# Pool sums over 8 and 16 tokens by one running-sum scan in place of three or four doubling additions

## The chip, the cores and the metric

The kernel runs on one core of one Trainium2 chip. The metric is device time in microseconds (us), the median over runs of one launch. In what follows PE is the matrix engine, DVE the vector engine, ACT the scalar engine, POOL the GpSimd engine, and SP the engine whose queue issues most of the DMA transfers. L12 means line 12 of the kernel before; lines of the changed kernel behind the edit are nine higher.

## What is computed

One layer of a hybrid decoder step. 2048 prompt tokens and 8 sequences of 8 sampled tokens (2112 tokens, 1024 features) are normalised and multiplied by `w_in` into four groups of 1024 columns: pool input `v`, pool gate, LRU input and LRU gate. The LRU group runs a convolution of width 4 and a gated recurrence; the pool group, which the change concerns, subtracts each token from a causal mean over its window and applies a 256x256 matrix per channel group:

```python
POOL_WINDOWS = (2, 4, 8, 16)      # one window per group of 256 channels
...
ext = jnp.concatenate([buf, v], axis=1)              # 15 rows of state, then the tokens
cs0 = concat([zeros, jnp.cumsum(ext, axis=1)], axis=1)
hi = cs0[:, POOL_BUF + 1:POOL_BUF + 1 + T, c0:c1]
lo = cs0[:, POOL_BUF + 1 - w:POOL_BUF + 1 - w + T, c0:c1]
cnt = jnp.minimum(pos + 1, w)
outs.append((hi - lo) / cnt - xcur[:, :, c0:c1])
...
y = jnp.einsum('btgc,gcd->btgd', d, pool_w) * pool_scale
```

Both groups are multiplied by SiLU of their gates, go through `w_out`, are normalised again and are added to the input.

## The kernel before, in words

Channels lie on the 128 partitions and tokens along the free dimension. Every fp32 operand of a matmul is split into a high and a low part (`hi` by a copy on ACT, `lo` by a subtraction on DVE), and each product takes three matmuls. The tokens are cut into three macro chunks m = 0, 1, 2 of 704 tokens; m = 2 also holds the 64 sampled tokens, which with their state rows make its pool rows 839 long instead of 719. In each macro chunk the work goes by quads: (m, p, kind), p = 0 to 3, kind V (pool input), G (pool gate), U (LRU input), L (LRU gate). A quad is a 256-column piece of the input projection for both halves of the chunk.

For m = 0 a quad is computed plainly, in eight steps. For m = 1 and 2 it is computed by seven products of 12 matmuls (a fast form of 2x2 block multiplication), numbered pid 1 to 7. Each needs one operand made of weight blocks (`w1V_4` is the one for m = 1, kind V, pid 4) and one made of the chunk's inputs. The seven input operands X11, T1, T2, X22, X21, T3, T4 lie in the big tile `XN`; pid 1, 5, 6, 3, 2, 7, 4 read them in this order. T1 to T4 are sums and differences ("raw" parts, written by DVE into `XA` or into two tiles `t_0`, `t_1`), and each of the seven then needs its `hi` (ACT, L334 or L336) and its `lo` (DVE, L321) before PE can use it. All seven are made anew at the two passages from one macro chunk to the next (`transition`, L1338). The pids 1, 6, 7 and 4 of a quad accumulate into one PSUM bank called `a`, and DVE or ACT reads the bank out after each (evacuation, L1007 on DVE), so pid 4 cannot start before pid 7 has been read out.

The pool input of a quad V lands in two tiles `e` (one per 128 channels), with 15 older tokens in front. When a quad V is complete, `pool_chain` (L1075) forms the window sums on DVE: for a window w it adds the tile to itself shifted by 1, 2, 4, ... (`tadd`, L324), each addition into a tile `s` of its own; that is one, two, three and four additions per tile for w = 2, 4, 8, 16. Then L1107 makes the mean minus the token, ACT and DVE split it into `dh` and `dl`, and PE applies the group's matrix (`y`), whose result DVE multiplies with the gate (L1153).

The order of the instructions on every engine is written by a small planner in the kernel itself, at build time: a generator such as `pool_chain` yields the engine that its next piece needs and the piece's cost in us, and the planner places the pieces against its own clock between the steps of the projection (`one_slot`, `run_jobs`). A piece whose result is needed at once is placed by `force`, just ahead of the product that needs it (`need_x`, L1385, for the inputs; `need_w` for the weights). Each engine then executes its instructions strictly in that order. The costs that `pool_chain` yields therefore move other work as well, on all engines. The planner also counts the tiles `e`, of which there are six (`e_free`).

After the three chunks follows the output projection in a fixed order (from L1803), which the change leaves alone.

Of the kernel before, what the change touches and what calls it, by code (L numbers as in the profile page):

```python
# [14 lines left out]
ALU = mybir.AluOpType  # L15
# [14 lines left out]
PB = 15  # L30
# [43 lines left out]
def hymba_kernel(  # L74
# [27 lines left out]
    def t_free():  # L102
        return T_BUFS - t_live[0]
# [5 lines left out]
    e_live = [0]  # L109

    def e_free():
        return E_BUFS - e_live[0]

    def e_tile(name, dtype=F32):
        e_live[0] += 1
        return sb.tile([P, EW], dtype, tag="e", bufs=E_BUFS, name=name)
# [90 lines left out]
    V, G, AC = nc.vector, nc.gpsimd, nc.scalar  # L207
# [52 lines left out]
    def seq8(ap, base, stride, off, n):  # L260
        return ap[:, base:base + N_S * stride].rearrange("p (s t) -> p s t", t=stride)[:, :, off:off + n]

    def as8(ap):
        return ap.rearrange("p (s t) -> p s t", t=S_S)
# [55 lines left out]
    def tsub(out, a, b, eng=None):  # L320
        (eng or V).tensor_tensor(out=out, in0=a, in1=b, op=ALU.subtract)  # L321

    def tadd(out, a, b, eng=None):
        (eng or V).tensor_tensor(out=out, in0=a, in1=b, op=ALU.add)  # L324
# [21 lines left out]
    def blocks(kind, p):  # L346
        return [KINDS[kind] + 2 * p + j for j in range(2)]
# [583 lines left out]
    def load_small(m, kind, p):  # L931
        t = sb.tile([P, 2, 512], F32R, tag=kind, bufs=1, name=f"{kind}{m}_{p}")
        small[kind] = t
        flat = t.rearrange("p a b -> p (a b)").bitcast(F32)
        i = 0 if kind == "pw" else 1
        if m:
            nc.sync.dma_start(out=flat, in_=swd[:, i, p, :])
            return
        if (kind, p) not in small_raw:
            small_early(kind, p)  # L940
        r = small_raw.pop((kind, p))

        def work():
            yield "A", 0.62
            AC.copy(out=t[:, 0, :], in_=r)
            yield "V", 0.71
            tsub(t[:, 1, :], r, t[:, 0, :].bitcast(F32))
            t_done(1)
            yield "t", LAG
            yield "D", 0  # L950
            nc.sync.dma_start(out=swd[:, i, p, :], in_=flat)
        small[kind, "job"] = spawn(work(), rank=1)
# [99 lines left out]
    def quad_end(q):  # L1052
        at = clock["A"] + HOP
        if q[2] in "GL":
            spawn(silu_chain(q), at, rank=1)
        elif q[2] == "V":
            spawn(pool_chain(q), at, rank=1)
        else:
            for j in range(2):
                spawn(conv_chain(q, j), at, rank=2)  # L1060
# [14 lines left out]
    def pool_chain(q):  # L1075
        m, p, _ = q
        w = WINDOWS[p]
        L = PB + MW if m < LM else PB + PW + N_S * SP_ST
        c = L * 0.00122 + 0.05
        ds = []  # L1080
        for j, blk in enumerate(blocks("V", p)):
            E = Q[q]["dst"][j]
            yield "G", 0.3
            if m < LM:
                G.tensor_copy(out=hp[:, blk, :], in_=E[:, MW:MW + PB])
            else:
                op = sb.tile([P, N_S + 1, PB], F32, tag="op", bufs=1, name=f"op{blk}")
                G.tensor_copy(out=op[:, 0, :], in_=E[:, PW:PW + PB])
                G.tensor_copy(out=op[:, 1:, :], in_=seq8(E, PB + PW, SP_ST, S_S, PB))
                nc.sync.dma_start(out=o_pool[blk], in_=op)  # L1090
            S, sh = E, 1
            while sh < w:
                yield "?", lambda: e_free() >= 1
                yield "V", c
                dst = e_tile(f"s{blk}_{m}_{sh}")
                first = PB if 2 * sh == w else 2 * sh - 1
                tadd(dst[:, first:L], S[:, first:L], S[:, first - sh:L - sh])
                if sh > 1:
                    e_live[0] -= 1
                S, sh = dst, 2 * sh  # L1100
            yield "V", 0.92
            if m == 0:
                f = sb.tile([P, 16], F32, tag="df", bufs=1, name=f"df{blk}")
                V.tensor_tensor(out=f[:, :w - 1], in0=S[:, PB:PB + w - 1], in1=rcnt[:, :w - 1], op=ALU.mult)
            d, e = S[:, PB:PB + MW], E[:, PB:PB + MW]
            n = MW if m < LM else PW
            V.scalar_tensor_tensor(out=d[:, :n], in0=d[:, :n], scalar=1.0 / w, in1=e[:, :n],  # L1107
                                   op0=ALU.mult, op1=ALU.subtract)
            if m == LM:
                V.scalar_tensor_tensor(out=as8(d[:, PW:MW]), in0=seq8(S, PB + PW, SP_ST, PB, S_S), scalar=1.0 / w,  # L1110
                                       in1=seq8(E, PB + PW, SP_ST, PB, S_S), op0=ALU.mult, op1=ALU.subtract)
            if m == 0:
                tsub(d[:, :w - 1], f[:, :w - 1], e[:, :w - 1])
            ds.append(d)
            e_live[0] -= 1
        Q[q]["d"] = []
        prev = Q.get((m, p - 1, "V") if p else (m - 1, NG - 1, "V"))
        yield "?", lambda: not prev or prev.get("maps")
        if not m and not p:
            yield "?", lambda: t_free() >= 1  # L1120
        load_small(m, "pw", p)
        for j, d in enumerate(ds):
            yield "A", 0.78
            dh = e_tile(f"dh{m}_{p}{j}", F32R)[:, :MW]
            AC.copy(out=dh, in_=d)
            yield "?", lambda: e_free() >= 1
            yield "V", 0.9
            dl = e_tile(f"dl{m}_{p}{j}", F32R)[:, :MW]
            tsub(dl, d, dh.bitcast(F32))
            e_live[0] -= 1  # L1130
            Q[q]["d"].append((dh, dl))
        sums.add((m, p))
        yield "?", lambda: Q.get((m, p, "G"), {}).get("silu")
        yield "t", 1.5
        for c in range(2):
            for j in range(2):
                yield "P", lambda j=j, c=c: pool_map(q, j, c)

    def pool_map(q, j, c):
        m, p, _ = q  # L1140
        need_small("pw")
        pw = small["pw"]
        Y = z_psum(f"y{m}{p}{j}{c}")[:, :CW]
        cs = slice(c * CW, (c + 1) * CW)
        mm3(Y, [(pw[:, 0, 256 * k + P * j:256 * k + P * (j + 1)], pw[:, 1, 256 * k + P * j:256 * k + P * (j + 1)],
                 Q[q]["d"][k][0][:, cs], Q[q]["d"][k][1][:, cs]) for k in range(2)])
        blk = 2 * p + j
        g = Q[m, p, "G"]["dst"][j]
        if j and c:
            Q[q]["maps"] = True  # L1150

        def evac():
            V.scalar_tensor_tensor(out=g[:, cs], in0=Y, scalar=col(C_SCALE, blk), in1=g[:, cs],  # L1153
                                   op0=ALU.mult, op1=ALU.mult)
            if c == 1:
                if j == 1:
                    e_live[0] -= 4

                def store():
                    yield "t", MLAG  # L1160
                    yield "D", 0
                    nc.gpsimd.dma_start(out=mixed[:, blk, m * MW:(m + 1) * MW], in_=g[:, :MW])  # L1162
                    t_done(1)
                spawn(store(), clock["V"] + HOP)
        return [("V", 0.58, evac)]
# [359 lines left out]
    with tc.manual_schedule():  # L1525
# [132 lines left out]
        clock.update(V=2.0, A=2.0, G=1.0)  # L1658
        T[0] = 0.0
        spawn(pool_chain((0, 0, "V")), rank=1)  # L1660
        spawn(silu_chain((0, 0, "G")), rank=1)
        for j in range(2):
# [56 lines left out]
        for n, (qi, i, qp, pid) in enumerate(slots):  # L1719
            q = QUADS[qi]  # L1720
            m = q[0]
# [210 lines left out]
```

## Time and profile before

| what | value |
|---|---|
| three runs | 1164.01, 1159.36 and 1167.0 us, median 1164.01 us |
| the profiled execution: its own time | 1162.96 us |
| its span in the profile | 1161.3 us |
| granted PE clock, mean | 0.996 |
| PE busy | 1125.8 us (97%) |
| DVE busy | 839.6 us (72%) |
| ACT busy | 656.5 us (57%) |
| POOL busy | 156.2 us (13%) |

The profile is that of one execution; times inside it count from the start of its span. Busy time is the time in which an engine executed something. The waits of an engine name what ended each of its idle times. A matmul of 352 columns is listed with 0.32 us, but matmuls overlap: twelve of them, listed together with 2.12 us, start 1.95 us before the next twelve.

### The profile page before, as it was taken

The numbers are of one execution on the slowest core, as the hardware profiler recorded it, in microseconds if no ns is written. First come the engines' busy times: TensorE is split into PE (matmuls) and PEld (weight loads), VectorE is DVE, ScalarE is ACT, GpSimd is POOL, SyncE is SP. The second block draws the span as 40 slices with busy tenths as digits, with TensorE's granted clock in tenths as the row PEclk, the third lists the DMA queues.
The fourth block names the chain that finished last, engine by engine and source line by source line (L and its number), as shares of the span: only waits on it lengthen the run. The fifth ranks groups of instructions, "written<-read, shape, count | busy, mean of one in ns | idle before, by whom it ended". The sixth has DMA issues, their size and how long they took to land. (4 is left out here: it accounts for less than half of the span.)

```text
span 1161.3 us, 17773 instructions
## 1 busy us (share of the span) xinstructions
PE 1125.8 (97%) x6274; PEld 1053.5 (91%) x6274; DVE 839.6 (72%) x1341; ACT 656.5 (57%) x1113; POOL 156.2 (13%) x264
## 2 busy tenths in 40 slices
PE   7999999999999999989899999999999999999996
PEld 6999999999999999989899999899888888888875
DVE  6797694779957656579767676656576578778777
ACT  5378666687784737568464847374864242344232
POOL 4201101001101010101202010101000003211232
PEclk9999999999999999999999999999999999999998
DMA  9655976976977989997999999998789577776563
GB/s 328 232 210 212 348 263 257 359 283 210 361 279 270 334 301 335 373 367 268 346 308 398 363 362 368 347 339 276 223 227 266 160 209 214 205 230 195 163 182 126
DMA packets 177464, 322.10 MB, mean 277 GB/s; under 512 B 24736, under 2 KB 86432, under 8 KB 177376
## 3 DMA queue, kind: packets, MB, share of 16 engines
q1 hardware_dynamic: 173536, 303.67, 76.3%
q0 software_dynamic: 3840, 17.30, 3.8%
q8 instruction: 49, 0.80, 0.3%
q14 instruction: 39, 0.32, 0.1%
HBM read 218.51 MB, written 102.15 MB: 276 GB/s over the span
## 5 line engine op out<-in xcount | busy, mean ns | idle before, releaser
L149 ACT ACT_TABLE_LOAD x70 | 89.8, 1283 | 2.0 <-PEq L1911 0.8
L458 PE MATMUL p<-XN,s 128*128 128x512 f32 (+1 forms) x224 | 86.9, 388 | 0.4 <-DVE s L141 0.4
L457 PE MATMUL p<-XN,s 128*128 128x512 f32 (+1 forms) x224 | 86.8, 387 | 0.0
L456 PE MATMUL p<-XN,s 128*128 128x512 f32 (+1 forms) x224 | 86.8, 387 | 0.0
L1190 DVE SCALAR_TENSOR_TENSOR xs<-u,parT,xs 128x704 f32<-128x704 f32 (+1 forms) x72 | 67.8, 956 | 18.4 <-ACT xs L1179 18.2
L449 POOL TENSOR_TENSOR xr<-ac,xr 128x512 f32<-128x512 f32 x27 | 49.0, 1835 | 214.9 <-DVE ac L590 110.9
L1153 DVE SCALAR_TENSOR_TENSOR g<-y,parT,g 128x352 f32<-128x352 f32 x48 | 27.9, 581 | 52.8 <-PE y L251 52.6
L569 ACT ACTIVATE p<-ac 128x512 f32<-128x512 f32 (+1 forms) x32 | 18.8, 587 | 83.0 <-DVE ac L449 83.0
L251 PE MATMUL zL<-XN,wL 128*128 128x352 f32 x384 | 64.9, 325 | 0.6 <-DVE wL L321 0.6
L251 PEld LDWEIGHTS zL<-XN,wL 128*128 128x128 f32 x384 | 62.6, 188 | 1.1 <-DVE wL L321 1.1
L138 ACT CAST s<-a 128x512 fp32r<-128x512 f32 x48 | 28.6, 616 | 49.5 <-DVE a L449 37.1
L449 DVE TENSOR_TENSOR a<-a,a 128x512 f32<-128x512 f32 x48 | 33.0, 690 | 31.9 <-DMA a<-mixed 28.7
L1162 POOL DMA_DIRECT2D mixed<-g x24 | 13.1, 548 | 306.2 <-DVE g L1153 117.2
L457 PE MATMUL p<-XN,a 128*128 128x512 f32 x137 | 54.2, 396 | 0.0
L456 PE MATMUL p<-XN,a 128*128 128x512 f32 x137 | 54.2, 395 | 0.0
L458 PE MATMUL p<-XN,a 128*128 128x512 f32 x137 | 54.2, 395 | 0.0
L251 PE MATMUL y<-dh,pw 128*128 128x352 f32 x192 | 54.1, 323 | 0.0
L458 PEld LDWEIGHTS p<-XN,s 128*128 128x128 f32 x224 | 42.1, 188 | 10.3 <-DVE s L141 0.8
L457 PEld LDWEIGHTS p<-XN,s 128*128 128x128 f32 x224 | 42.1, 188 | 9.5
L456 PEld LDWEIGHTS p<-XN,s 128*128 128x128 f32 x224 | 42.1, 188 | 9.4
L251 PE MATMUL zV<-XN,wV 128*128 128x352 f32 x288 | 48.6, 324 | 0.0
L251 PE MATMUL zG<-XN,wG 128*128 128x352 f32 x288 | 48.2, 324 | 0.0
(341 smaller groups left out, 3134.2 us busy)
## 6 DMA issues: line engine op xcount, KB each, us to landing
a<-mixed SPq DMA_DIRECT2D x112, 256.0 KB, 3.9
mixed<-g POOLq DMA_DIRECT2D x48, 352.0 KB, 6.1
w2V<-wsd SPq DMA_DIRECT2D x28, 512.0 KB, 6.7
w2G<-wsd SPq DMA_DIRECT2D x28, 512.0 KB, 6.9
w2U<-wsd SPq DMA_DIRECT2D x28, 512.0 KB, 6.7
w2L<-wsd SPq DMA_DIRECT2D x28, 512.0 KB, 7.6
wsd<-XN SPq DMA_DIRECT2D x27, 512.0 KB, 5.0
w1V<-wsd SPq DMA_DIRECT2D x24, 512.0 KB, 6.8
```

The lines of the kernel that those rows point to most:

```text
L138: hi_eng.copy(out=hi, in_=src)
L149: nc.scalar.preload_act_table_set(name)
L251: nc.tensor.matmul(out, lhsT=lhsT, rhs=rhs, start=start, stop=stop)
L449: (eng or nc.vector).tensor_tensor(out=out, in0=a, in1=b, op=op)
L456: nc.tensor.matmul(out, lhsT=ah, rhs=wh, start=start and k == 0, stop=False)
L457: nc.tensor.matmul(out, lhsT=ah, rhs=wl, start=False, stop=False)
L458: nc.tensor.matmul(out, lhsT=al, rhs=wh, start=False, stop=stop and k == KT - 1)
L569: nc.scalar.activation(out=junk, in_=o, func=AF.Square, accum_out=st[:, g:g + 1])
L1153: V.scalar_tensor_tensor(out=g[:, cs], in0=Y, scalar=col(C_SCALE, blk), in1=g[:, cs], op0=ALU.mult, op1=ALU.mult)
L1162: nc.gpsimd.dma_start(out=mixed[:, blk, m * MW:(m + 1) * MW], in_=g[:, :MW])
L1190: V.scalar_tensor_tensor(out=xs, in0=E[:, k:k + n], scalar=col(C_CW + 8 * k, b), in1=xs, op0=ALU.mult, op1=ALU.add)
```

## The change

For the windows 8 and 16 the loop of additions is replaced by two instructions: a reduction adds the first window (the w tokens that end with the chunk's first), and a scan carries it on, adding at each token the one that enters the window and subtracting the one that leaves it. The pieces yield 2.0 us of DVE to the planner in place of three or four times about 0.93 us (1.07 us for m = 2). One tile `s` is taken in place of three or four. The windows 2 and 4 keep their additions.

```diff
-            S, sh = E, 1
-            while sh < w:
+            if w > 4:
                 yield "?", lambda: e_free() >= 1
-                yield "V", c
-                dst = e_tile(f"s{blk}_{m}_{sh}")
-                first = PB if 2 * sh == w else 2 * sh - 1
-                tadd(dst[:, first:L], S[:, first:L], S[:, first - sh:L - sh])
-                if sh > 1:
-                    e_live[0] -= 1
-                S, sh = dst, 2 * sh
+                yield "V", 2.0
+                S = e_tile(f"s{blk}_{m}")
+                V.tensor_reduce(out=S[:, PB:PB + 1], in_=E[:, PB + 1 - w:PB + 1], axis=mybir.AxisListType.X,
+                                op=ALU.add)
+                V.tensor_tensor_scan(out=S[:, PB + 1:L], data0=E[:, PB + 1:L], data1=E[:, PB + 1 - w:L - w],
+                                     initial=S[:, PB:PB + 1], op0=ALU.add, op1=ALU.subtract)
+            else:
+                S, sh = E, 1
+                while sh < w:
+                    yield "?", lambda: e_free() >= 1
+                    yield "V", c
+                    dst = e_tile(f"s{blk}_{m}_{sh}")
+                    first = PB if 2 * sh == w else 2 * sh - 1
+                    tadd(dst[:, first:L], S[:, first:L], S[:, first - sh:L - sh])
+                    if sh > 1:
+                        e_live[0] -= 1
+                    S, sh = dst, 2 * sh
```

With the other costs the planner places much of DVE's, ACT's and PE's work between about 200 us and 800 us in another order. On PE the products of the projection keep their order; the gate products (`r`, `i`) and the pool products (`y`) between them move by up to about a dozen products, and pid 4 of two V quads changes its place. In the middle chunk (m = 1, p = 1) pid 4 now follows directly on pid 7, where two products of the G quad stood between them; in the last chunk (m = 2, p = 1) it is the other way round. The places below matter most. All three are on DVE. The numbers behind the names count instances and differ between the two programs for the same thing; `wr1G` to `w1G` are steps that make weight operands.

The first is the passage from m = 0 to m = 1, around pid 3, 2 and 7 of the first V quad (the evacuations `e1V`, `d1V` and `a1V`). Before:

```order
L321 TENSOR_TENSOR XN<-XA,XN 128x1408
L321 TENSOR_TENSOR wr1G_21_2994<-wr1G_11_2990,wr1G_21_2994 128x512
L321 TENSOR_TENSOR w1G_5_3184<-wr1G_22_2996,w1G_5_3184 128x512
L321 TENSOR_TENSOR wr1G_11_2990<-wr1G_22_2996,wr1G_11_2990 128x512
L1007 TENSOR_TENSOR e_1_3145<-e1V_3170,e_1_3145 128x352
L321 TENSOR_TENSOR wr1G_12_2992<-wr1G_12_2992,wr1G_11_2990 128x512
L321 TENSOR_TENSOR w1G_6_3222<-wr1G_11_2990,w1G_6_3222 128x512
L1007 TENSOR_TENSOR e_1_3145<-d1V_3229,e_1_3145 128x352
L321 TENSOR_TENSOR w1G_3_3243<-wr1G_12_2992,w1G_3_3243 128x512
L321 TENSOR_TENSOR xl_0_3168<-xs_0_3015,xh_0_3167 128x704
L1007 TENSOR_TENSOR e_1_3147<-a1V_3149,e_1_3147 128x352
```

In the changed kernel, the same stretch:

```order
L321 TENSOR_TENSOR XA<-XA 128x2x352 x2
L1007 TENSOR_TENSOR e_1_3123<-e1V_3145,e_1_3123 128x352
L321 TENSOR_TENSOR XN<-XA,XN 128x1408
L1007 TENSOR_TENSOR e_1_3123<-d1V_3203,e_1_3123 128x352
L324 TENSOR_TENSOR wr1G_22_2970<-wr1G_21_2968,wr1G_22_2970 128x512
L321 TENSOR_TENSOR w1G_5_3159<-wr1G_22_2970,w1G_5_3159 128x512
L1007 TENSOR_TENSOR e_1_3125<-a1V_3127,e_1_3125 128x352
L321 TENSOR_TENSOR XN<-XA,XN 128x1408
```

The first row of the piece before is the last of the seven `lo` parts, T4's, which pid 4 reads; it stood ahead of all three evacuations. Now the sixth (T3's) stands behind that of `e1V` and the seventh (T4's) behind that of `a1V`.

The second place is the passage from m = 1 to m = 2, around the same evacuations of its first V quad. Before:

```order
L1190 SCALAR_TENSOR_TENSOR xs_1_5760<-u_1_5449,parT,xs_1_5760 128x704
L321 TENSOR_TENSOR XA<-XA 128x2x352 x2
L1007 TENSOR_TENSOR e_2_5780<-e2V_5808,e_2_5780 128x288
L1007 TENSOR_TENSOR e_2_5780<-e2V_5808,e_2_5780 128x8x8
L321 TENSOR_TENSOR t_0_5711<-XA,t_0_5711 128x704
L321 TENSOR_TENSOR t_1_5712<-XA,t_1_5712 128x704
L321 TENSOR_TENSOR XN<-XA,XN 128x1408
L1007 TENSOR_TENSOR e_2_5780<-d2V_5881,e_2_5780 128x352
L1007 TENSOR_TENSOR e_2_5783<-a2V_5786,e_2_5783 128x288
L1007 TENSOR_TENSOR e_2_5783<-a2V_5786,e_2_5783 128x8x8
L321 TENSOR_TENSOR XN<-t_0_5711,XN 128x704
L321 TENSOR_TENSOR XN<-t_1_5712,XN 128x704
```

In the changed kernel:

```order
L1199 SCALAR_TENSOR_TENSOR xs_1_5687<-u_1_5420,parT,xs_1_5687 128x704
L1007 TENSOR_TENSOR e_2_5746<-e2V_5773,e_2_5746 128x288
L1007 TENSOR_TENSOR e_2_5746<-e2V_5773,e_2_5746 128x8x8
L321 TENSOR_TENSOR XA<-XA 128x2x352 x2
L321 TENSOR_TENSOR XN<-XA,XN 128x1408
L1007 TENSOR_TENSOR e_2_5746<-d2V_5846,e_2_5746 128x352
L1007 TENSOR_TENSOR e_2_5749<-a2V_5752,e_2_5749 128x288
L1007 TENSOR_TENSOR e_2_5749<-a2V_5752,e_2_5749 128x8x8
L321 TENSOR_TENSOR t_0_5706<-XA,t_0_5706 128x704
L321 TENSOR_TENSOR t_1_5707<-XA,t_1_5707 128x704
L321 TENSOR_TENSOR XN<-t_0_5706,XN 128x704
L321 TENSOR_TENSOR XN<-t_1_5707,XN 128x704
```

The raw part of T3 (`XA<-XA`) moved from ahead of the evacuation of `e2V` to behind it, and the raw part of T4 (`t_0`, `t_1`) from ahead of the evacuation of `a2V` to behind it, so that all three steps of T4 follow that evacuation.

The third place is the last G quad of m = 1, where DVE evacuates `d1G` and `a1G` and also computes the norm of the next chunk's tokens (`tok`, L293 to L299; one of its steps waits for a root on ACT). Before:

```order
L324 TENSOR_TENSOR s_1_8_5250<-s_1_4_5246 128x704
L1007 TENSOR_TENSOR g_1_5076<-d1G_5218,g_1_5076 128x352
L1107 SCALAR_TENSOR_TENSOR s_1_8_5250<-s_1_8_5250,e_1_4919 128x704
L293 TENSOR_SCALAR tok<-tok 128x6
L296 RECIPROCAL tok<-tok 128x6
L297 TENSOR_TENSOR tok<-tok 128x6
L298 SCALAR_TENSOR_TENSOR tok<-tok 128x6
L299 SCALAR_TENSOR_TENSOR tok<-tok 128x6
L1007 TENSOR_TENSOR g_1_5077<-a1G_5078,g_1_5077 128x352
```

In the changed kernel:

```order
L1007 TENSOR_TENSOR g_1_5053<-d1G_5193,g_1_5053 128x352
L1095 TENSOR_REDUCE s_1_5244<-e_1_4923 128x1
L1097 SCALAR_TENSOR_TENSOR s_1_5244<-e_1_4923,s_1_5244 128x703
L1007 TENSOR_TENSOR g_1_5054<-a1G_5055,g_1_5054 128x352
L321 TENSOR_TENSOR w1L_7_5263<-wr1L_21_5080,w1L_7_5263 128x512
L293 TENSOR_SCALAR tok<-tok 128x6
```

The evacuation of `a1G` moved ahead of the norm's steps; between the two evacuations now stand the reduction and the scan (printed as SCALAR_TENSOR_TENSOR at L1097).

## The prediction

> **What bounds the kernel now.** First the busy line of PE, then the busy times by window.
>
> ```profile
> PE 1125.8 (97%) x6274; PEld 1053.5 (91%) x6274; DVE 839.6 (72%) x1341; ACT 656.5 (57%) x1113; POOL 156.2 (13%) x264
> ```
>
> ```profile
> 262.00:311.00 49.00, 48.28 (x296) 47.74 (x295) 46.55 (x60) 36.32 (x52) 5.87 (x9) 1.00 0.76 269
> ...
> 100.00:800.00 700.00, 685.60 (x4200) 680.55 (x4199) 502.46 (x732) 450.56 (x711) 74.15 (x180) 1.00 0.88 320
> ```
>
> The window rows give length, then busy time of PE, weight loads, DVE, ACT and POOL. PE bounds the kernel: of the 700 us in which all pool sums lie, it works 685.6 at the full granted clock (the 1.00 behind the engines). The change adds or removes no matmul, so it can move only the 14.4 us in which PE stands there, or add to them. DVE is busy for 502 of the 700 us, so most of its work is hidden; but at the first passage between macro chunks (262 to 311 us) it is busy for 46.55 of 49 us, and there its order counts. Next the waits of PE, with their totals, counts and longest.
>
> ```profile
> PE a1G L249 <- DVE g L1007: 2.2, 1, 2.2
> ...
> PE a2V L249 <- DVE XN L321: 2.2, 2, 1.9
> ...
> PE e2V L249 <- DVE XN L321: 1.0, 1, 1.0
> ...
> PE a1V L249 <- DVE e L1007: 0.7, 1, 0.7
> ```
>
> PE's waits for DVE in the stretch come to 2.2 + 2.2 + 1.0 + 0.7 = 6.1 us: one evacuation of the last G quad of m = 1, the inputs of the second passage, and one evacuation of the first. That is the most that a less loaded DVE can give back; the other 8 us end with DMA, ACT or at no releaser that is shown.
>
> **The change on DVE.** The groups of L324 are the additions; L1256 is the recurrence's scan over about the same length, once with its start value in SBUF; L581 and L579 are operations on one column. Each row ends in busy us and mean ns of one.
>
> ```profile
> L1256 DVE TENSOR_TENSOR_SCAN rg<-w,hh,ig 128x728 f32<-128x728 f32 x8 | 13.9, 1732 | 0.2
> L1256 DVE TENSOR_TENSOR_SCAN rg<-w,hh,ig 128x704 f32<-128x704 f32 x8 | 13.4, 1679 | 0.1
> ...
> L324 DVE TENSOR_TENSOR s<-e 128x718 f32<-128x718 f32 x12 | 10.8, 899 | 0.0
> ...
> L324 DVE TENSOR_TENSOR s<-s 128x704 f32<-128x704 f32 x12 | 10.6, 882 | 0.0
> ...
> L324 DVE TENSOR_TENSOR s<-s 128x716 f32<-128x716 f32 x8 | 7.2, 896 | 0.0
> ...
> L324 DVE TENSOR_TENSOR s<-e 128x838 f32<-128x838 f32 x6 | 6.2, 1035 | 0.0
> ...
> L581 DVE TENSOR_SCALAR st<-st 128x1 f32<-128x1 f32 x16 | 4.4, 273 | 0.5
> ...
> L579 DVE TENSOR_SCALAR st<-st 128x1 f32<-128x1 f32 x16 | 2.5, 154 | 0.5
> ```
>
> Removed are 8 x 3 additions or 4 each for m = 0 and 1 (two chunks, two tiles, windows 8 and 16): 4 x 3 + 4 x 4 = 28 at about 0.89 us, and for m = 2 2 x 3 + 2 x 4 = 14 at about 1.03 us: 24.9 + 14.4 = 39.3 us. Added are 12 reductions of at most 16 elements and 12 scans. No reduction of this kind stands in the trace; the one-column rows bound it at 0.15 and 0.27 us, and I take 0.2. The scan of 703 gets the row of 704 with a start value in SBUF, 1.68 us. From 704 to 728 it grows by 53 ns, 2.2 ns per element, so that of 823 takes 1.68 + 119 x 0.0022 = 1.94 us. No scan with an add and a subtract is in the trace: below, it might cost as much as an addition of that length (0.88 us), above, twice the scan of the rows (3.4 us); I take 1.68, the same operation with other arithmetic. Added: 12 x 0.2 + 8 x 1.68 + 4 x 1.94 = 23.6 us. DVE saves about 16 us, at the scan's bounds 26 or, when it doubles, minus 5. All of it lies beside PE's work, so it enters the sum only where PE waits for DVE. A scan is one piece of 1.7 us where evacuations could slip between additions of 0.9, so an evacuation that falls due behind it comes up to 0.8 us later; PE notices only where pid 4 follows directly on pid 7. The reduction reads the 15 older tokens that POOL wrote when the quad began, as the first addition did, so POOL's queue holds it no longer than before; SP issues the same loads, and fewer tiles `s` are in use.
>
> The scan's row is 1.90 times the addition's on the same 704 elements (1679 against 882 ns). [...]
>
> In the timeline an addition of 0.89 us lets its successor begin after 0.81:
>
> ```profile
> 502.87 0.89 DVE L324 TENSOR_TENSOR s<-s 128x712 f32<-128x712 f32 x1
> 503.68 0.69 DVE L321 TENSOR_TENSOR w1L<-wr1L,w1L 128x512 fp32r<-128x512 f32 x1
> ```
>
> So 18 instructions fewer save some 1.5 us less than their durations say, about 14 us. [...]
>
> **What moves, first passage.** PE's products and DVE's rows there:
>
> ```profile
> 305.39 2.11 PE L249 MATMUL a1V<-XN,w1V 128*128 128x352 f32 x12
> 308.22 2.21 PE L249 MATMUL a1V<-XN,w1V 128*128 128x352 f32 x12 [0.72 <-DVE e L1007]
> ```
>
> ```profile
> 299.50 1.62 DVE L321 TENSOR_TENSOR XN<-XA,XN 128x1408 fp32r<-128x1408 f32 x1
> ...
> 307.65 0.52 DVE L1007 TENSOR_TENSOR e<-a1V,e 128x352 f32<-128x352 f32 x1
> ```
>
> Pid 7 ends at 307.50, its evacuation at 308.17, and pid 4 begins at 308.22; T4's low part was ready at 301.12. In the changed order that part follows the evacuation. Of pid 4 only the first matmul (0.16 us) can run without it. So PE goes on 308.1 + 1.62 = 309.7 at the earliest: 2.2 us after pid 7, less 0.16, is 2.0 in place of 0.72. T3's low part, now behind the evacuation of pid 3, ends some 2.1 us after it, a product takes 1.95, which adds 0.2 to 0.4. Term: **+1.6 us**; below 0 if DVE's queue lets the part through early, above 2.7 if ACT's high part of T4 is late by another 1 us.
>
> **Second passage.**
>
> ```profile
> 554.92 2.05 PE L249 MATMUL e2V<-XN,w2V 128*128 128x352 f32 x11 [1.01 <-DVE XN L321]
> ...
> 562.64 2.11 PE L249 MATMUL d2V<-XN,w2V 128*128 128x352 f32 x12
> 564.59 0.33 PE L249 MATMUL a2V<-XN,w2V 128*128 128x352 f32 x1
> 566.78 2.05 PE L249 MATMUL a2V<-XN,w2V 128*128 128x352 f32 x11 [1.87 <-DVE XN L321]
> 569.56 0.40 PE L249 MATMUL a2V<-XN,w2V 128*128 128x352 f32 x1 [0.73 <-issue]
> 570.31 2.04 PE L249 MATMUL a2V<-XN,w2V 128*128 128x352 f32 x11 [0.35 <-DVE XN L321]
> ```
>
> ```profile
> 562.91 0.59 DVE L1007 TENSOR_TENSOR e<-e2V,e 128x288 f32<-128x288 f32 x2 [2.44 <-PE e2V L249]
> 563.42 1.68 DVE L321 TENSOR_TENSOR t<-XA,t 128x704 f32<-128x704 f32 x2
> 565.02 1.70 DVE L321 TENSOR_TENSOR XN<-XA,XN 128x1408 fp32r<-128x1408 f32 x1
> ...
> 569.37 1.69 DVE L321 TENSOR_TENSOR XN<-t,XN 128x704 fp32r<-128x704 f32 x2
> ```
>
> ```profile
> 562.49 1.37 ACT L336 CAST XN<-XA 128x1408 fp32r<-128x1408 f32 x1
> ```
>
> T3: now the evacuation of pid 3 (0.5), the raw part (1.7), ACT's high part (1.37) and the low part (1.65) follow one another, 5.2 us, while PE has a product of 1.95 and one matmul to do: a wait of 3.1 in place of 1.87, +1.2. T4: the evacuation of pid 7 (0.5), the raw part (1.6) and the first half of the low part (0.85, with 0.1 to hand over) make 3.05, less one matmul 2.9, in place of 0.73 + 0.35: +1.8. T1's low part (the 1.01) now stands a product earlier and costs nothing; T2's stands later, behind two other low parts, and comes about 0.2 late. Term: +1.2 + 1.8 - 1.0 + 0.2 = **+2.2 us**, between -1 (the parts run ahead after all) and +5 (ACT is late for T2 and T3 by 1.4 us each).
>
> **Evacuations and pid 4.**
>
> ```profile
> 508.10 2.21 PE L249 MATMUL a1G<-XN,w1G 128*128 128x352 f32 x12 [2.24 <-DVE g L1007]
> ```
>
> ```profile
> 505.51 0.89 DVE L1107 SCALAR_TENSOR_TENSOR s<-s,e 128x704 f32<-128x704 f32 x1
> ...
> 507.53 0.52 DVE L1007 TENSOR_TENSOR g<-a1G,g 128x352 f32<-128x352 f32 x1
> ```
>
> ```profile
> 620.78 2.17 PE L249 MATMUL a2V<-XN,w2V 128*128 128x352 f32 x12 [1.70 <-DMA w2V<-wsd]
> ```
>
> Between 505.51 and 507.53 DVE made a mean and the tokens' norm before it evacuated `a1G`; in the changed order a reduction and a scan (1.9 us) stand there, but three or four additions less stand ahead. The evacuation comes some 2 us earlier: **-2.0**, of 2.24 at most. The 1.70 us ended with the load of `w2V_4`, at a pid 4 directly behind pid 7; two products later, that load is no longer late: -1.7. The like pair now made in m = 1 costs at least the 0.7 of an evacuation and at most that 1.7; I take 1.2. Net **-0.5**.
>
> **Sum:** +1.6 + 2.2 - 2.0 - 0.5 = +1.3 us on a profiled execution of 1162.96 us (a span of 1161.3 and 1.7 around it), 1164.3 us. The median of the runs shown is 1.05 us above that execution; with the same sum it would become 1165.3. Between the two I predict **1165 us**: no change.
>
> **Rivals.** *The savings reach the end.* If DVE set the pace, its 14 us would come off: 1163 - 14 = 1149 us, faster by 1.2%. For it speaks the 95% at the first passage; against it that PE waits for DVE for 6.1 us in all. A milder form, in which all these waits go and the pair at 620.78 too, gives 1163 - 6.1 - 1.7 = 1155 us, still within 1%.
>
> *The passages are made on demand.* The mechanism of T3 and T4 takes hold of every combination: each then costs raw part, high part and low part, 1.7 + 1.37 + 1.65 = 4.7, less a product of 1.95, so 2.75 us, for four of them at two passages 22 us, less the 4 us of waits that stand there already: 1163 + 18 = 1181 us, slower by 1.6%. It decides from the point at which the low part of T1 or T2, too, stands behind the evacuation just before its use. The order shows this for T4 at both passages and for T3 at the second, not for T1 and T2; but DVE may arrive late at them.
>
> *The scan is no cheaper.* At 3.4 us a scan DVE would lose 5 us and stay at 73%; four evacuations wait up to 1.7 us longer behind a scan: 1163 + 1.3 + 4 x 1.0, about 1168 us, within 1%.
>
> **How the numbers follow.** About 1% (11.6 us) is what a measurement of this kernel can tell from no change; its three runs alone lie 7.6 us apart. Chances: the forecast 0.65; the mild relief 0.12; the scan no cheaper 0.08; the savings reach the end 0.06; passages on demand 0.09. Within 1%: 0.65 + 0.12 + 0.08 = 0.85; faster 0.06; slower 0.09. The terms' own bounds add up to -4 (0 - 1 - 2.2 - 1.0) and +9 (2.7 + 5 + 0 + 1.7), so 1159 to 1172 us; with 3 us more on either side for the place of a new median among runs 7.6 us apart, the range is 1156 to 1175 us. It leaves out the savings that reach the end, most of the passages on demand and the edge of the mild relief.
>
> **What would show it.** Right: 12 scans near 1.7 and 1.9 us; DVE busy about 825 us; PE busy within 1 us of 1125.8; the wait at `a1G` gone; waits of PE of 2 us for T4 at the first passage, and of about 3 us each for T3 and T4 at the second; no wait for `w2V_4` at 620. Wrong: a wait of PE over 3 us that is not at the passages; passages whose waits stay at 0.7 and 4; PE's idle time between 100 and 800 us below 8 or above 26 us.

## The result, and the profile after

The changed kernel takes 1168.54 us (median of 16 runs, 1164.68 to 1172.25) where before took 1163.1 us beside it (16 runs, 1157.85 to 1167.0): 1.0053 times as long, 95% interval 1.0037 to 1.0069. It is slower by half a per cent, some 6 us. The forecast was 1165 us and no change that can be told; the time lies inside the range, but the loss is four to five times the 1.3 us of the sum. The profiled execution of the changed kernel is the longest of its 16 (1172.25 us, span 1170.5 us), so what is read in it overstates the loss: 9.2 us of span against before's profile. Of all kernels below, two executions in a slower state (1226.6 us at price 2.5, 3453.5 us at price 0.8) are left out of medians and ratios.

The busy line of the page, after:

```profile
PE 1129.9 (97%) x6274; PEld 1056.9 (90%) x6274; DVE 823.9 (70%) x1323; ACT 651.1 (56%) x1108; POOL 165.9 (14%) x264
```

The new instructions by their lines (count, then shortest, median and longest duration in ns):

```profile
L1097 DVE TENSOR_TENSOR_SCAN s<-e,s x12: 1681/1682/1931, 154.4 to 770.9; 128x703 f32<-128x703 f32 x8, 128x823 f32<-128x823 f32 x4
L1095 DVE TENSOR_REDUCE s<-e x12: 150/154/167, 154.2 to 770.7; 128x1 f32<-128x8 f32 x6, 128x1 f32<-128x16 f32 x6
```

DVE does 15.7 us less (839.6 to 823.9), as the prices of the prediction said. In other pairs of profiles that differ by scan for additions alone it is 12.5 to 16.5 us, so the 16 us and the 14 us of the prediction can't be told apart. PE, which runs the same matmuls, is busy for 4.1 us more: some of its matmuls took longer. Where, the products of PE show. First passage, after (start, duration; in brackets the idle time ahead and what ended it):

```profile
298.89 0.32 PE L249 MATMUL a1V<-XN,w1V 128*128 128x352 f32 x1
300.41 2.05 PE L249 MATMUL a1V<-XN,w1V 128*128 128x352 f32 x11 [1.20 <-DVE XN L321]
...
309.52 0.40 PE L249 MATMUL a1V<-XN,w1V 128*128 128x352 f32 x1 [0.84 <-issue]
311.00 3.52 PE L249 MATMUL a1V<-XN,w1V 128*128 128x352 f32 x11 [1.09 <-DVE XN L321]
```

PE waits for T2's low part (1.20), then at pid 4 until pid 7 is read out (0.84; DVE ends that evacuation at 309.42), then for T4's low part (1.09); before there was one wait of 0.72. And the eleven matmuls at 311.00 took 3.52 us instead of 2.05. Second passage, after:

```profile
553.61 2.12 PE L249 MATMUL a2V<-XN,w2V 128*128 128x352 f32 x12
...
561.07 2.18 PE L249 MATMUL a2V<-XN,w2V 128*128 128x352 f32 x12 [1.43 <-DMA w2V<-wsd]
563.09 2.11 PE L249 MATMUL e2V<-XN,w2V 128*128 128x352 f32 x12
565.04 2.11 PE L249 MATMUL d2V<-XN,w2V 128*128 128x352 f32 x12
568.95 0.43 PE L249 MATMUL a2V<-XN,w2V 128*128 128x352 f32 x1 [1.80 <-ACT XN L336]
570.61 3.42 PE L249 MATMUL a2V<-XN,w2V 128*128 128x352 f32 x11 [1.23 <-DVE XN L321]
576.31 0.43 PE L249 MATMUL a2V<-XN,w2V 128*128 128x352 f32 x1 [2.29 <-ACT XN L334]
577.24 3.51 PE L249 MATMUL a2V<-XN,w2V 128*128 128x352 f32 x11 [0.50 <-DVE XN L321]
...
588.40 2.12 PE L249 MATMUL d2G<-XN,w2G 128*128 128x352 f32 x12
```

Here PE waits 1.80 + 1.23 = 3.03 us for T3 and 2.29 + 0.50 = 2.79 us for T4, and twice more eleven matmuls take 3.4 to 3.5 us. DVE at that place shows the new order: the raw part of T3 (565.81) stands behind the evacuation of `e2V`, and DVE was idle for 3.70 us before that evacuation.

```profile
565.31 0.59 DVE L1007 TENSOR_TENSOR e<-e2V,e 128x288 f32<-128x288 f32 x2 [3.70 <-PE e2V L249]
565.81 1.68 DVE L321 TENSOR_TENSOR XA<-XA 128x704 f32<-128x704 f32 x2
568.93 1.62 DVE L321 TENSOR_TENSOR XN<-XA,XN 128x1408 fp32r<-128x1408 f32 x1 [1.43 <-ACT XN L336]
```

The long matmuls stand where the granted clock is recorded at 0.50. Rows of 3.41 us, the length of each stretch at 0.50, after (length, busy time of PE, weight loads, DVE, ACT, POOL, then the clock):

```profile
307.47:310.88 3.41, 1.60 (x9) 1.10 (x7) 2.72 (x5) 0.62 (x1) 0.00 (x0) 1.00 0.34 126
310.88:314.30 3.42, 3.30 (x11) 3.30 (x12) 3.39 (x6) 0.00 (x0) 0.00 (x0) 0.50 0.95 266
314.30:317.71 3.41, 3.41 (x23) 3.41 (x22) 1.79 (x4) 2.46 (x5) 0.57 (x1) 1.00 0.84 238
...
566.88:570.30 3.42, 0.70 (x3) 0.19 (x1) 1.99 (x2) 1.36 (x1) 0.76 (x1) 1.00 1.03 414
570.30:573.71 3.41, 3.10 (x11) 3.11 (x11) 0.69 (x2) 0.00 (x0) 0.00 (x0) 0.50 1.01 404
573.71:577.12 3.41, 0.74 (x3) 0.22 (x2) 3.02 (x6) 1.56 (x2) 0.00 (x0) 1.00 0.65 184
577.12:580.54 3.42, 3.30 (x11) 3.30 (x12) 3.42 (x5) 0.00 (x0) 0.00 (x0) 0.50 0.18 71
```

Three times a row in which PE worked for 1.60, 0.70 or 0.74 us of 3.41 is followed by one at clock 0.50. Each costs 1.4 to 1.5 us (3.52, 3.42 and 3.51 in place of 2.05), 4.3 us together. In the profile of before the clock stays at 1.00 at both passages (250 to 320 and 540 to 600 us); around its longest wait there (1.87 us, for T3) PE worked for 1.94 us of a row:

```profile
565.31:568.72 3.41, 1.94 (x11) 1.75 (x11) 1.85 (x2) 0.60 (x1) 0.00 (x0) 1.00 1.02 418
```

How much a passage costs can be read in one number, since twelve products lie between the first product of the second passage and `d2G`: 588.40 - 553.61 = 34.79 us after, 580.03 - 551.62 = 28.41 us before, and 12 x 1.955 = 23.5 us if PE never waited (from 563.09 to 565.04, where it does not, the starts lie 1.95 us apart). Before:

```profile
551.62 2.12 PE L249 MATMUL a2V<-XN,w2V 128*128 128x352 f32 x12
...
580.03 2.12 PE L249 MATMUL d2G<-XN,w2G 128*128 128x352 f32 x12
```

Some of the other waits of PE, after, with total, count and longest:

```profile
PE a2L L249 <- DMA w2L<-wsd: 3.1, 2, 2.0
...
PE a2G L249 <- DMA w2G<-wsd: 1.7, 1, 1.7
PE p L458 <- DVE s L141: 1.4, 1, 1.4
PE a1G L249 <- DVE g L1007: 1.3, 1, 1.3
```

### The profile page after: what moved, and what is told of

The parts are those of the page before. It is cut to its first block, busy times and chain, and to the rows that moved or that the text cites. A ratio compares the mean times of both kernels' runs of the same rounds, so it can differ in the third digit from the quotient of the medians.

```text
span 1170.5 us, 17746 instructions
## 1 busy us (share of the span) xinstructions
PE 1129.9 (97%) x6274; PEld 1056.9 (90%) x6274; DVE 823.9 (70%) x1323; ACT 651.1 (56%) x1108; POOL 165.9 (14%) x264
## 5 line engine op out<-in xcount | busy, mean ns | idle before, releaser
L251 PE MATMUL zU<-XN,wU 128*128 128x352 f32 x288 | 48.4, 324 | 0.0
```

The source lines that it names most:

```text
L251: nc.tensor.matmul(out, lhsT=lhsT, rhs=rhs, start=start, stop=stop)
```

## The experiments

The theory to be tested: the scan costs nothing; the order that the planner makes of the new price costs, chiefly at the passages, and the waits there halve PE's clock. Rivals: the scan costs as one long piece on DVE; the clock falls whatever PE does; the order makes no difference. Ratios are to before, run beside each on the same chip. Beside the kernels of the experiments its median was 1160.4 to 1161.5 us, not 1163.1, so rows are to be compared by their ratios and not by their medians. "Clock" is the median over a kernel's runs of the mean granted clock (before: 0.995 over 86 runs; the change: 0.991 over 16). "Second passage" is the profile's time for the twelve products; with price 2.2 six short gate products lie among them, about 1 us, and in the filled kernels the matmuls that were added.

| kernel | median us | ratio, 95% interval | clock | second passage us |
|---|---|---|---|---|
| before | 1163.1 | 1 | 0.995 | 28.41 |
| the change | 1168.54 | 1.0053 [1.0037, 1.0069] | 0.991 | 34.79 |
| scan, order of before | 1164.46 | 1.0032 [1.0012, 1.0051] | 0.993 | 32.15 |
| additions, order of the change | 1174.46 | 1.0125 [1.0107, 1.0142] | 0.990 | 34.64 |
| the change, PE filled | 1165.85 | 1.0046 [1.0029, 1.0062] | 0.995 | 31.27 |
| sums left out, order of before | 1162.03 | 1.0014 [0.9996, 1.0032] | 0.994 | 28.39 |
| scan, price 1.8 | 1157.21 | 0.9970 [0.9950, 0.9990] | 0.996 | 33.76 |
| scan, price 2.2 | 1161.64 | 1.0002 [0.9987, 1.0017] | 0.993 | 34.42 |
| scan, price 2.5 | 1164.57 | 1.0020 [0.9999, 1.0040] | 0.994 | 33.68 |
| scan, three steps of 0.9 | 1150.67 | 0.9915 [0.9892, 0.9938] | 0.996 | 24.19 |
| additions, order of three steps | 1151.74 | 0.9921 [0.9899, 0.9942] | 0.996 | 24.15 |
| additions, price 0.8 | 1154.88 | 0.9941 [0.9920, 0.9963] | 0.995 | 25.92 |
| scan, order of before, PE filled | 1159.76 | 1.0003 [0.9983, 1.0022] | 0.995 | 28.41 |
| before, two instructions moved | 1159.93 | 0.9994 [0.9977, 1.0011] | 0.994 | 27.14 |

**The scan in the order of before.** The planner's steps stay; the pair (reduction and scan) is issued in the last one. In the traces every other instruction of PE, DVE, ACT and POOL stands in the same order as before.

```diff
             while sh < w:
                 yield "?", lambda: e_free() >= 1
                 yield "V", c
+                if w > 4:
+                    e_live[0] += 1
+                    if 2 * sh == w:
+                        e_live[0] -= 1
+                        S = e_tile(f"s{blk}_{m}")
+                        V.tensor_reduce(...)
+                        V.tensor_tensor_scan(...)
+                    if sh > 1:
+                        e_live[0] -= 1
+                    sh *= 2
+                    continue
```

> The scan in the order of before: the planner is asked for the three or four steps of before at their old price, and reduction and scan are issued in the last of them; all other instructions stand where they stood before, on every engine. Theory (the loss comes from the order that the single step of 2.0 gives): no slower than before, 1159 to 1163 us; DVE busy about 824 us; PE's waits 0.7 us at the first passage and about 4 us at the second, as before, and no window of half clock between 250 and 620 us. Rival (the scan itself costs, as one piece of 1.7 us that evacuations stand behind): 1166 to 1170 us, as the change.

Slower than before by 0.3%, 4 us against the before that ran beside it, and between the two expectations: DVE's relief brought nothing here, and neither answer is right as it stands. The profile shows where the relief went. DVE and PE of this kernel, ahead of the second passage:

```profile
511.49 0.69 DVE L324 TENSOR_TENSOR wr1U<-wr1U,wr1U 128x512 f32<-128x512 f32 x1 [5.25 <-DMA wr1U<-in_w_in]
```

```profile
504.10 2.22 PE L249 MATMUL a1G<-XN,w1G 128*128 128x352 f32 x12 [1.13 <-DVE g L1007]
...
515.56 2.84 PE L249 MATMUL a1L<-XN,w1L 128*128 128x352 f32 x12 [1.66 <-ACT g L1011]
518.19 3.06 PE L249 MATMUL a1U<-XN,w1U 128*128 128x352 f32 x12
```

and ACT:

```profile
512.26 0.62 ACT L845 CAST w1U<-wr1U 128x512 fp32r<-128x512 f32 x1 [5.46 <-DVE wr1U L324]
...
515.08 0.43 ACT L1011 COPY g<-a1L 128x352 f32<-128x352 f32 x1
```

`a1G` starts 4.0 us earlier than in before (504.10 against 508.10). But the raw weights `wr1U` do not come earlier by as much: DVE starts on them at 511.49, 2.8 us earlier than in before (514.32), and waits 5.25 us for them (1.63 in before), ACT behind it 5.46, the evacuation of `a1L` stands behind that on ACT, and PE waits for it 1.66 us (0.45 in before). At the second passage the lead is 1.3 us (`a2V` at 550.31 against 551.62). With the wait PE worked for 1.76 of the 3.42 us of a row, and in the next the clock was 0.53 in the mean. At the second passage a row with 1.79 us of work is followed by two at 0.50 and 0.53:

```profile
513.63:517.05 3.42, 1.76 (x11) 1.62 (x12) 3.38 (x6) 3.41 (x6) 0.00 (x0) 0.97 0.79 249
517.05:520.46 3.41, 3.41 (x14) 3.41 (x14) 2.92 (x5) 2.63 (x6) 0.00 (x0) 0.53 1.00 369
564.83:568.25 3.42, 1.79 (x10) 1.56 (x10) 2.43 (x3) 1.17 (x2) 0.51 (x1) 0.97 1.03 417
568.25:571.66 3.41, 2.56 (x8) 1.76 (x7) 2.10 (x4) 0.00 (x0) 0.00 (x0) 0.50 1.02 416
571.66:575.07 3.41, 3.41 (x14) 3.41 (x13) 3.41 (x5) 0.43 (x1) 0.89 (x1) 0.53 0.84 303
```

The second passage took 32.15 us in the same order in which before took 28.41. PE's waits there, 4.2 us, are hardly longer than before's 4.0; the row of before with 1.94 us of work was followed by clock 1.00. So of the 3.7 us at this passage some 3.5 are longer matmuls, and not longer waits.

**The sums left out.** As before, but the mean takes `E` in place of the sum and no addition or scan is made for windows 8 and 16.

> The order of before with no sums over 8 and 16 tokens at all: additions and scan are left out, and the mean is taken of the tokens themselves. DVE has 39 us less than before. Theory (DVE's work on the sums lies beside PE's): 1157 to 1163 us, at most the 6 us of PE's waits for DVE. Rival (DVE sets the pace where the sums stand): 1150 us or less.

DVE did 34 us less (805.2 us busy) and nothing came of it: 1.0014, with 1 in the interval. The rival that the savings reach the end is gone, for this order. The same loads hold it up again: DVE's idle time for `wr1U`, and PE's wait behind it, grew further:

```profile
512.41 0.69 DVE L324 TENSOR_TENSOR wr1U<-wr1U,wr1U 128x512 f32<-128x512 f32 x1 [6.92 <-DMA wr1U<-in_w_in]
```

```profile
516.48 3.89 PE L249 MATMUL a1L<-XN,w1L 128*128 128x352 f32 x12 [3.02 <-ACT g L1011]
```

**The additions in the order of the change.**

```diff
             if w > 4:
                 yield "?", lambda: e_free() >= 1
                 yield "V", 2.0
-                S = e_tile(f"s{blk}_{m}")
-                V.tensor_reduce(...)
-                V.tensor_tensor_scan(...)
+                S, sh = E, 1
+                while sh < w:
+                    ...
```

> The doubling additions in the order of the change: one step of 2.0 to the planner, and the three or four additions issued in it; all other instructions stand as in the change. Theory (the order costs): as slow as the change or slower, 1167 to 1175 us, since DVE is 16 us busier in the same order; the waits of PE at the second passage 7 us or more. Rival (the scan costs): 1163 us, as before.

1.25% slower than before: the order alone, with before's own additions, costs 14 us, and in it the scan ends 8 us earlier than the additions. So the scan does help where DVE is late; the largest single wait shows it (1.31 us in the change):

```profile
511.96 3.66 PE L249 MATMUL a1G<-XN,w1G 128*128 128x352 f32 x12 [4.59 <-DVE g L1007]
```

**PE filled.** Matmuls with a weight tile of zeros add nothing to the bank, but keep PE at work (18.70 of 20.00 us and 48.53 of 50.00 us in the two rows below).

```diff
+    FILL = {(1, 0, 'V', 6): (0, 6), (1, 0, 'V', 4): (0, 6), (2, 0, 'V', 6): (6, 0), (2, 0, 'V', 7): (9, 6), (2, 0, 'V', 4): (9, 2)}
+    ...
+    def fillers(out, n):
+        for _ in range(n):
+            mm(out, zero, xq("X11", 0, 0), False, False, True)
+
     def quad_product(...):
+        fillers(out, fill[0])
         for k in range(HK):
             mm(out, wh, xh, start and k == 0, False, chain)
+            if k == 0:
+                fillers(out, fill[1])
```

> The change, with 44 matmuls more on PE at the five places of the two passages where it waits: products with weights of zero, added to the bank that the next product uses (0.16 us each by the rows of 12 in 1.95 us, 7 us in all), so that PE works where it stood. Theory (the half clock of 3.4 us at the passages follows from PE standing about half of a window): the granted clock stays at 1.00 from 300 to 320 and from 550 to 600 us, the products there take 2.1 us again, and the end comes 2 to 4 us earlier than the change, 1164 to 1167 us. Rival (the clock falls whatever PE does): drops as in the change, and 1168 to 1172 us with what the added matmuls cost.

The clock does what the theory says at the passages, so the rival that it falls whatever PE does is gone. Stretches of this kernel:

```profile
300.00:320.00 20.00, 18.70 (x111) 17.56 (x110) 17.08 (x23) 8.04 (x14) 2.49 (x3) 1.00 0.76 267
550.00:600.00 50.00, 48.53 (x294) 47.18 (x293) 34.11 (x45) 20.87 (x39) 7.88 (x14) 1.00 0.92 324
```

Both passages run at 1.00, the second takes 3.5 us less than in the change, and the clock over its runs is back at before's 0.995 (in the profile a row at 0.50 stands behind them, 719.67 to 723.08 us, after one with 1.02 us of work in 3.41). In the total less is left: 1.0046 against 1.0053, intervals that overlap, so a gain in time is not shown. The 44 matmuls take PE about 7 us themselves (an estimate, 44 x 0.16, from twelve in 1.95 us), in place of waits and past them.

**The scan in the order of before, PE filled**, with ten such matmuls ahead of the wait at 515 us and eight inside T3's product.

```diff
+    FILL = {(1, 2, 'L', 2): (0, 0, 10), (2, 0, 'V', 7): (0, 8, 0)}
```

> The scan in the order of before, with 18 matmuls by weights of zero on PE: 10 behind the last product ahead of the wait at 515 us, 8 inside the product of T3 at the second passage. Theory (4 us were lost there, the larger half of it to two stretches of half clock): no stretch of half clock at 517 and 568 us, and 1161 to 1163 us, 2 us less than without them. Rival (the scan as a long piece on DVE costs it): 1164 to 1166 us.

Neither of the two stretches of half clock is left (the clock is 1.00 from 510 to 520 and from 560 to 576 us), and the ratio falls from 1.0032 to 1.0003. This kernel is as fast as before, with more on PE. That fits the reading that the clock took what the scan seemed to cost in that order, but does not prove it: the two intervals still overlap (1.0012 to 1.0051 and 0.9983 to 1.0022). The kernel's profiled run is one of its longest (1167.05 us), because of one load late by 4.69 us at 621 us.

**Other prices.** The one step's price is 2.0 in the change; here 1.8, 2.2 and 2.5, then three steps of 0.9 with the pair behind the third.

```diff
-                yield "V", 2.0
+                yield "V", 1.8
```

> The change with 1.8 in place of 2.0 as the one step's price to the planner, which gives another order; the same instructions in all. At the first passage the low parts of T3 and T4 stand ahead of the evacuations, as before; at the second they stand as in the change. Theory (the order costs, above all at the passages): between the two, 1162 to 1166 us, waits of the first passage 0.7 us again, those of the second 5 to 7. Rival (a price near the scan's true time is all that matters, or the one piece costs): as the change, within 2 us.

> The change with 2.2 as the step's price. At the first passage T4's low part stands behind the evacuations, as in the change; at the second the raw sums of T3 and T4 are made before the low parts of T1 and T2, ahead of where they stood in either kernel. Theory (the order costs): 1162 to 1167 us, waits of about 3 us at the first passage, under 5 at the second. Rival: as the change, within 2 us.

> The change with 2.5 as the step's price. Both passages stand as in the change, much else on PE stands otherwise. Theory (the passages carry the loss): as the change, 1166 to 1171 us, waits of 3 and 7 us, and stretches of half clock there. Rival (the loss is spread over the whole order, and passages are a part of it only): anywhere from 1158 to 1175 us.

> The change with three steps of 0.9 ahead of the reduction and the scan for either window. The first passage stands as before; at the second T4's raw sum is made ahead of T2's low part, earlier than in either kernel. Theory (the order costs, above all at the passages): 1159 to 1163 us, no more than before, waits of 0.7 us and of 4 us at most. Rival: as the change, 1166 to 1170 us.

In two of these expectations tiles are misnamed: at the second passage it is T3's raw part that stands ahead of T2's low part with three steps (T4's is next behind it), and with 2.2 the raw parts of T2 and T3 stand ahead of the low parts of T1 and T2.

The same instructions in five orders range from 0.9915 to 1.0053, with no trend by price. Price 1.8 came out below its range: its second passage is as bad as the change's (33.76 us), but at the first pid 4 stands behind two products of G and no wait is left: 21.56 us from the first `a1V` to `d1G`, 27.22 in the change. Price 2.5, with passages like the change's (27.27 us for 27.22 at the first, 33.68 for 34.79 at the second), missed its range by 1.4 us, so the rest of the order seems to have a part too. Price 2.2 had no wait at the first passage, pid 4 again standing behind two products of G, and lost 7.22 us in one wait for T1's low part at the second: both against its expectation, and the time within it. Three steps give the fastest kernel of all, 0.85% under before, and better than was expected. From 100 to 800 us PE stands 4.9 us in it, 14.4 in before and 18.3 in the change. Its second passage, PE and DVE:

```profile
558.91 2.11 PE L249 MATMUL d2V<-XN,w2V 128*128 128x352 f32 x12
560.86 0.33 PE L249 MATMUL a2V<-XN,w2V 128*128 128x352 f32 x1
561.36 2.05 PE L249 MATMUL a2V<-XN,w2V 128*128 128x352 f32 x11 [0.17 <-DVE XN L321]
563.24 2.10 PE L249 MATMUL a2G<-XN,w2G 128*128 128x352 f32 x12
565.18 2.12 PE L249 MATMUL e2G<-XN,w2G 128*128 128x352 f32 x12
567.14 2.12 PE L249 MATMUL a2V<-XN,w2V 128*128 128x352 f32 x12
```

```profile
552.53 1.69 DVE L321 TENSOR_TENSOR XA<-XA 128x704 f32<-128x704 f32 x2
554.14 1.69 DVE L321 TENSOR_TENSOR XN<-t,XN 128x704 fp32r<-128x704 f32 x2
555.74 1.69 DVE L321 TENSOR_TENSOR t<-XA,t 128x704 f32<-128x704 f32 x2
559.18 0.59 DVE L1007 TENSOR_TENSOR e<-e2V,e 128x288 f32<-128x288 f32 x2 [1.75 <-PE e2V L249]
559.68 1.62 DVE L321 TENSOR_TENSOR XN<-XA,XN 128x1408 fp32r<-128x1408 f32 x1
```

Both raw parts (552.53, 555.74) are made ahead of the evacuation of `e2V`, so that T3's low part follows that evacuation directly; and pid 4 comes two products of G after pid 7. One wait of 0.17 us is left, and the twelve products take 24.19 us.

**Whose gain is it?** The additions in that same order, and before with nothing but another price for its additions:

```diff
-                yield "V", c
+                yield "V", c if w <= 4 else 0.8
```

> The doubling additions in the order of the version with three steps of 0.9 (1150.7 us with the scan): all other instructions stand as there. It tells what the scan is worth in that order. If the order gives the gain: 1150 to 1155 us, faster than before all the same. If the scan gives it (16 us less on DVE): 1161 us or more. In the order of the change the same exchange was worth 8 us, in that of before nothing.

> Before, with nothing changed but the price of an addition for windows 8 and 16 told to the planner: 0.8 each in place of 0.93 (1.1 for m = 2). No scan. The first passage stands as before; at the second T4's raw sum stands ahead of T2's low part, as in the version with three steps. Theory (the second passage and the order at large carry the differences, scan or not): faster than before by 3 to 8 us, 1153 to 1158. Rival (the order is neutral and the scan gave the gain): 1161 us, as before.

The additions are as fast in that order as the scan (0.9921 and 0.9915, intervals that overlap almost wholly), with DVE 16 us busier. And a new price alone makes the kernel of before 0.6% faster, about 7 us: 2.5 of them at the second passage (25.92 for 28.41; T3's raw part is again the one that was meant), the rest elsewhere. The gain is the order's.

**Two instructions moved.** In before, the two instructions of T4's raw part are placed ahead of the evacuation of pid 3; all else stands.

```diff
         force(x_jobs[n])
+        if m == 2 and n == "X22":
+            while "T4" not in x_jobs:
+                run_jobs(T[0])
+                job = x_jobs["sums"]
+                if "T4" not in x_jobs and job["req"][0] == "V":
+                    grant(job, max(clock["V"], job["ready"], T[0]))
```

> Before, additions and all, with one thing changed: the two instructions of DVE that make T4's raw sum at the second passage stand ahead of the evacuation of pid 3 (where DVE stood idle for 2.44 us in before) and not behind it. Every other instruction stands as before on every engine. Theory (the place of the operands' instructions at the passages sets PE's wait there): T3's low part ends 1.6 us earlier, PE's wait for it falls from 1.87 to about 0.3 us, and the end comes 1.6 us earlier or more, 1157 to 1160 us where before has 1161. Rival (later gates take it back, as at 515 us): 1161 us.

```profile
562.73 0.33 PE L249 MATMUL a2V<-XN,w2V 128*128 128x352 f32 x1
563.71 2.04 PE L249 MATMUL a2V<-XN,w2V 128*128 128x352 f32 x11 [0.66 <-DVE XN L321]
...
617.79 3.51 PE L249 MATMUL a2V<-XN,w2V 128*128 128x352 f32 x12 [1.81 <-DMA w2V<-wsd]
```

The wait for T3 falls from 1.87 to 0.66 us and the passage from 28.41 to 27.14, so the place of these instructions does set that wait. The total, 0.9994, does not tell a gain of 1.3 us from none, and the expected 1.6 us are not shown in it. The load of `w2V` at the pid 4 of the next V quad ends a wait of 1.81 us, 1.70 in before, and here the twelve matmuls behind it took 3.51 us where they took 2.17 in before.

## Why the prediction was right, and where its sum was not

- **PE bounds, and DVE's saving lies beside it: right.** Taking the additions' price off DVE by the scan (12.5 us in that profile), or the sums altogether (34 us), in before's order moved the time by +0.3% and +0.1%; in the order of three steps the scan moved it by less than the interval. Only in the order of the change, where DVE is late, did it bring 8 us. The saving by itself therefore did not reach the end, and the kernel became slower by its order.
- **The prices: right.** Scans of 1.68 and 1.93 us (taken 1.68 and 1.94), reductions 0.15 (0.2), DVE at 823.9 us ("about 825").
- **First passage, +1.6 us: the step taken was right, the term too small.** The wait at pid 4 was foreseen at 2.0, the readout of pid 7 included, and is 0.84 + 1.09 = 1.93. That T2's low part would come late by 1.20 was not foreseen. Measured: 3.13 us of waits for 0.72, +2.4.
- **Second passage, +2.2 us: right for T3 and T4** (3.1 and 2.9 foreseen, 3.03 and 2.79 measured), and T1's wait did go. A load of `w2V` for pid 6 (1.43) was not in the sum. Measured: 7.25 us of waits for 3.96, +3.3.
- **`a1G`, -2.0 us: half of it came**, 2.24 to 1.31.
- **Pairs of pid 7 and 4, -0.5 us:** the wait of 1.70 at 620 us went, and the pair now made in m = 1 costs 0.62 where 1.2 was taken. But waits for loads grew elsewhere (`a2G` from 1.0 to 1.7, `a2L` from 0.6 to 3.1), and at the output projection one grew by 1.0 us (`p`, 0.4 to 1.4). The sum counted a wait that goes as time saved; these other waits more than took it back, and why they grew was not tested.
- **The term that was missing: the clock.** The prediction said that PE works "at the full granted clock" and gave its drop no term. In the profiled run it is 4.3 us. Over all runs, a clock of 0.991 for 0.995 is 0.004 x 1165, about 4.7 us, the larger part of the 6 us lost; this estimate takes all of the lost clock as time in which PE had work. The scatter within kernels agrees with it: over 211 runs of all kernels, each set against its own kernel's medians, 0.001 less of clock goes with about 1 us more (one run of before, 1158.0 us at a recorded 0.947, does not fit and is left out). It is not proved: the filled kernel had before's clock, and its time did not come back.
- **PE's busy time "within 1 us of 1125.8": wrong**, 1129.9, for that reason. "A wait over 3 us off the passages": none came between 100 and 800 us, and PE's idle time there, 18.3 us, lies within the 8 to 26 that were named.
- **Rivals.** The savings that reach the end fell with the sums left out, and the scan that is no cheaper with its 1.68 us. The latter would have given about 1168 us, near the measured time, by a mechanism that is not there. Of the passages on demand, the waits for T3 and T4 are what was forecast, and T2 joined them at the first passage only.

So the verdict of no change within 1% rests on the right mechanisms, but the time lay inside the range partly by its width: the terms of the sum were too small together, and 16 runs do tell the half per cent that the prediction put below the 1% it took for measurable.

What stays open: why each order gains or loses outside the passages. Most of PE's waits there end with loads of weights, and no run held those loads fixed.

## What to carry to other kernels

Where a planner writes the order from told costs, an edit of one cost is a new draw of the whole order: compare the edit in one fixed order, both ways, before judging the operation. Here the operation was worth -8 to +4 us and the draw 23 us (0.9921 to 1.0125 with the same additions). On a kernel that keeps one engine at 97%, look for the few places where its operands are made just in time, and put their making ahead of readouts that must wait for that engine (here that shortened the wait, 1.87 to 0.66 us, though not measurably the whole); and count what a cluster of short waits does to the clock behind it (here 0.84 and 1.09 us, close together, stood ahead of 3.41 us at clock 0.50).

## What the runs showed of the hardware

The granted clock of PE is 1.00 in the profile of before from 19.2 to 1152 us. In that of the change it is 1.00 from 20 to 1164 us but for three stretches at 0.50, of 3.41 us each, which begin at 310.9, 570.3 and 577.1 us. What PE had worked in rows of 3.41 to 3.42 us, and the clock in the row that follows each:

| profile | row, us | PE worked, us | clock in the next row |
|---|---|---|---|
| additions, order of the change | 508.50 to 511.91 | 0.00 | 0.52 |
| the change | 566.88 to 570.30 | 0.70 | 0.50 |
| the change | 573.71 to 577.12 | 0.74 | 0.50 |
| the change, PE filled | 716.26 to 719.67 | 1.02 | 0.50 |
| the change | 307.47 to 310.88 | 1.60 | 0.50 |
| the change | 720.43 to 723.84 | 1.67 | 1.00 |
| scan, order of before | 513.63 to 517.05 | 1.76 | 0.53 |
| scan, order of before | 564.83 to 568.25 | 1.79 | 0.50 |
| scan, three steps of 0.9 | 503.89 to 507.30 | 1.80 | 1.00 |
| before | 565.31 to 568.72 | 1.94 | 1.00 |

So the five rows with 1.60 us of work or less were followed by 0.50 to 0.52, and of the five with 1.67 to 1.94 us two by 0.53 and 0.50. Ten rows show no sharper bound, and what a row holds hangs on where it is cut: 0.06 us earlier that of before holds 1.88 us. The waits of 0.84 and 1.09 us make up the rest of the row with 1.60 (the second ends 0.12 us behind it). Behind the three stretches of the change, in which PE worked for 3.30, 3.10 and 3.30 us, the clock was 1.00 again; with the scan in the order of before it was 0.53 behind a row at 0.50 with 2.56 us of work.

No kernel was profiled twice, but the mean clock of the change ranged from 0.988 to 0.994 over its 16 runs. An estimate from that: 0.006 of 1170 us is 7 us, as much as four stretches of 3.41 us at 0.50 lose, so the same order probably meets such a stretch in one run and not in the next.
